# Output projection by seven block products, with the gate sums moved into an earlier stage

## The chip, the cores and the metric

One core of a Trainium2 chip runs the whole kernel. The metric is the device time of one execution in microseconds, as the median of several runs; the kernel before takes 1436.12 us (1434.32 to 1437.77 in three runs).

## The reference, cut to what matters

The program is one decoder layer over 512 tokens of width 2048 in float32. An input `x` is normalised, scaled and shifted, and multiplied by a large input matrix. Its columns feed two branches, a causal convolution and a differential attention; each is gated and projected back to 2048 columns. The branches are merged by sigmoid gates. What the change touches is the end:

```python
merged = sigmoid(m_conv) * y_conv + sigmoid(m_attn) * y_attn     # 512 x 2048
out = merged @ w_o                                               # 2048 x 2048
gate = (silu(c) @ w_ada + b_ada)[4096:]                          # 2048 values
x = x + gate * rms_norm(out, g_post)
```

`rms_norm` divides each token's row by the root of its mean square and multiplies it by `g_post`.

## The kernel before, in words

Every float32 operand of a matmul is split into a high and a low part (`split`, lines 143 to 151): ScalarE casts the high part, VectorE subtracts it from the operand. `mm3` (line 165) then issues three matmuls, high by high, high by low and low by high.

A scheduler turns the written program into a fixed order for each engine; an operation may move ahead of earlier written ones when its operands and its buffer are there. Only operations marked `ordered` keep their written order among each other on TensorE. Side work is written as generators in the list `work`; `pump` runs a number of their steps between the products of the main work, so that VectorE's side work is spread.

The stages that matter come in this order. In the cz, ma and mc stages (664 to 1072 us) `gemm_blocks` multiplies by columns of `w_in` with seven block products in place of eight (Strassen's method in Winograd's form): `s1`, `s2`, `s3`, `s4` are sums of weight blocks, `T1`, `T2`, `T3`, `T4` of token blocks. After each product it calls `pump` for one step. The ya and yc stages (1072 to 1247 us, `gemm_y`) project the attention and the convolution branch; yc merges and splits the result into `mgs`. The output stage (from line 926) multiplies `mgs` by `w_o`, 512 columns (`n`) at a time: four token tiles of 128 in four PSUM banks, sixteen steps of 128 in the inner dimension, three matmuls each. The last column block keeps half of its weights split in SBUF, so that the token tiles end one after the other; each is then squared and summed, multiplied by `gate * g_post`, scaled by its root mean square and added to `x`.

`gate(n)` (line 874) computes 512 gate columns: it loads 16 blocks of `w_ada`, two at a time, VectorE multiplies each by the column's `silu(c)` and adds it up, and a matmul with ones (`pgt`) sums over the partitions. Gate 0 is in the list during the yc stage, gates 1 to 3 during the output stage.

Buffers are pools with a fixed number of tiles: 27 pages of 512 columns (`page`), 12 tiles `temp`, 3 buffers each for 1 MB of raw weights (`wr`, also used for `x` at the end), high parts (`wh`) and low parts (`wl`), 2 `ws`. PSUM has eight banks: four `g`, two `s`, one `t`, one `o`. All loads and stores go through SP's queue, in its order.

Of the kernel before, what the change touches and what calls it, by code (L numbers as in the profile page):

```python
# [9 lines left out]
F32 = mybir.dt.float32  # L10
F32R = mybir.dt.float32r
# [5 lines left out]
P = 128  # L17
# [34 lines left out]
def hybrid_trunk(ctx: ExitStack, tc: tile.TileContext, x, c, w_ada, b_ada, g_pre, g_post, w_in,  # L52
# [17 lines left out]
    def page(name, dt=F32):  # L70
        return pp.tile([P, S], dt, tag="pg", name=name)
# [38 lines left out]
    def small(n, name):  # L110
        return sp.tile([P, n], F32, tag=f"sm{n}", bufs=1 if n > 16 else 8, name=name)
# [328 lines left out]
    def temp(name, dt=F32):  # L440
        return mp.tile([P, S], dt, tag="tmp", bufs=NTEMP, name=name)
# [305 lines left out]
    def conv_stats():  # L747
# [82 lines left out]
    def gemm_y(src, c0, rhs, name):  # L830
        ps = [gbank(f"py_{name}_{f}") for f in range(2)]
        raw = wraw(src, 0, 8, c0, 256, name)
        for q0 in (0, 4):
            whi, wlo = wsplit(raw[:, q0:q0 + 4, :], f"{name}_{q0}")
            for k in range(4):
                for f in range(2):
                    fs = slice(f * P, (f + 1) * P)
                    mm3(ps[f], (whi[:, k, fs], wlo[:, k, fs]), rhs[q0 + k], q0 + k == 0, q0 + k == 7)
        return ps
# [29 lines left out]
        fetch(f"yal{k}", lo.bitcast(F32))  # L869
        ya.append((hi, lo))  # L870
    work.append(conv_norm())
    gg = []

    def gate(n):

        bg = temp(f"bg_{n}")
        nc.sync.dma_start(out=bg, in_=b_ada2[2 * D + n * 512:2 * D + (n + 1) * 512].partition_broadcast(P))
        gp = page(f"gg_{n}")
        nc.sync.dma_start(out=gp, in_=g_post[0][n * 512:(n + 1) * 512].partition_broadcast(P))
        acc = page(f"accg_{n}")  # L880
        for k0 in range(0, KT, 2):
            raw = mp.tile([P, 2, S], F32, tag="ws", bufs=2, name=f"adag_{n}_{k0}")
            nc.sync.dma_start(out=raw, in_=ada_v[:, k0:k0 + 2, 2 * D + n * 512:2 * D + (n + 1) * 512])
            for k in range(2):
                s1 = cact[:, k0 + k:k0 + k + 1]
                if k0 + k == 0:
                    nc.vector.tensor_scalar_mul(acc, raw[:, k, :], s1)
                else:
                    nc.vector.scalar_tensor_tensor(acc, raw[:, k, :], s1, acc, op0=ALU.mult, op1=ALU.add)  # L889
            yield  # L890
        pgt = gbank(f"pgt_{n}", "gt"[n % 2])
        nc.tensor.matmul(pgt, ones, acc, start=True, stop=True)
        nc.vector.tensor_tensor(bg, pgt, bg, op=ALU.add)
        nc.vector.tensor_tensor(gp, gp, bg, op=ALU.mult)
        gg.append(gp)

    for j in range(8):
        py = gemm_y(w_attn_out[0], j * 256, ya, f"ya{j}")
        for f in range(2):
# [6 lines left out]
            mg.append(g)  # L906
        pump(YP)
    pump()
    mgs = []
    work.append(gate(0))  # L910
    for j in range(8):
        py = gemm_y(w_conv_out[0], j * 256, yc, f"yc{j}")
        for f in range(2):
            k = 2 * j + f
            g = temp(f"ga_{k}")
# [14 lines left out]
    def out_evac(n, t, ps):  # L930
        sq = temp(f"fsq_{n}_{t}")
        nc.scalar.activation(sq, ps, AF.Square, accum_out=fss[:, 4 * t + n:4 * t + n + 1])  # L932
        og[t][n] = page(f"og_{n}_{t}")
        nc.vector.tensor_tensor(og[t][n], ps, gg[n], op=ALU.mult)

    def out_mm(ps, t, k, w):
        mh, ml = mgs[k]
        ts = slice(t * P, (t + 1) * P)
        mm3(ps, (mh[:, ts], ml[:, ts]), w, k == 0, k == KT - 1)

    res = []
    zp = small(4, "fzp")
    for n in range(4):
        if n < 3:
            work.append(gate(n + 1))
        ps = [gbank(f"pw_{n}_{t}", ("gggg", "ssto")[n % 2][t]) for t in range(NT)]
        for q0 in range(0, KT, 4):
            raw = wraw(w_o[0], q0, 4, n * 512, 512, f"o_{n}_{q0}")
            for q1 in (0, 2):
                k0 = q0 + q1  # L950
                if n == 3 and k0 >= KT - RES:
                    for k in range(q1, q1 + 2):
                        hi, lo = page(f"woh_{q0 + k}", F32R), temp(f"wol_{q0 + k}", F32R)
                        split(raw[:, k, :], hi, lo)
                        res.append((q0 + k, (hi, lo)))
                    continue
                whi, wlo = wsplit(raw[:, q1:q1 + 2, :], f"o_{n}_{k0}")
                pump(1)
                for k in range(2):
                    for t in range(NT):  # L960
                        out_mm(ps[t], t, k0 + k, (whi[:, k, :], wlo[:, k, :]))
        pump()
        if n < 3:
            for t in range(NT):
                out_evac(n, t, ps[t])

    nc.vector.reduce_sum(zp, fss.rearrange("p (t n) -> p t n", n=4)[:, :, :3], axis=mybir.AxisListType.X)
    nc.vector.tensor_scalar(zp, zp, 1.0 / D, 4.0 * EPS, op0=ALU.mult, op1=ALU.add)
    for t in range(NT):
        for k, w in res:  # L970
            out_mm(ps[t], t, k, w)
        out_evac(3, t, ps[t])
# [3 lines left out]
        nc.vector.scalar_tensor_tensor(z, fss[:, 4 * t + 3:4 * t + 4], 1.0 / D, zp[:, t:t + 1],
                                       op0=ALU.mult, op1=ALU.add)
        r = rsqrt1(z, f"fr_{t}")
        for a, b in ((0, 2), (2, 3), (3, 4)) if t == NT - 1 else ((0, 4),):
# [34 lines left out]
```

## Time and profile before

| what | us |
|---|---|
| median of three runs | 1436.12 |
| profiled execution, its own time | 1436.9 |
| its span | 1435.1 |
| TensorE busy | 1397.3 |
| VectorE busy | 1080.9 |
| ScalarE busy | 522.1 |
| DMA read and written | 238.62 MB, 166 GB/s |

The span is the time from the first to the last recorded instruction. A share of busy time is an average over stages; what a change in a stage is worth is read from that stage. Matmuls overlap in the record, so the time of one in a row of them is taken from the length of the row.

### The profile page before, as it was taken

How to read it: one execution, taken by the hardware profiler on the slowest of the kernel's cores; microseconds unless marked ns; L12 is line 12 of the kernel's file. 1: busy time of each engine (PE TensorE's matmuls, PEld its weight loads, DVE VectorE, ACT ScalarE, POOL GpSimd, SP SyncE). 2: the span in 40 equal slices, each digit the busy share in tenths (PEclk: the TensorE clock that was granted, in tenths of full speed). 3: DMA queues.
4: the chain of work that ended last, by engine and by line, in shares of the span. 5: the costliest groups of instructions: out<-in, count | busy, mean ns of one | idle time of the engine just before them, and what ended most of it. 6: DMA issues, size and time to landing. Idle time of an engine off the chain costs nothing.

```text
span 1435.1 us, 20362 instructions
## 1 busy us (share of the span) xinstructions
PE 1397.3 (97%) x7999; PEld 1189.5 (83%) x7999; DVE 1080.9 (75%) x1750; ACT 522.1 (36%) x839; POOL 1.8 (0%) x8
## 2 busy tenths in 40 slices
PE   5899999999999999999999999999999999999997
PEld 4676787887777867788999999999998888888885
DVE  6997976988888887588988878777767676526645
ACT  3421333223433244444544444444445223222230
POOL 0000000000000000000000000000000000000000
PEclk9999999999999999999999999999999999999999
DMA  9888732331322322234635655543369875236544
GB/s 301 288 280 304 237 123 92 125 121 59 117 67 96 103 67 84 86 111 142 224 128 192 198 170 174 172 140 121 134 233 350 280 243 181 88 107 231 190 147 147
DMA packets 178338, 238.62 MB, mean 166 GB/s; under 512 B 8689, under 2 KB 119618, under 8 KB 177346
## 3 DMA queue, kind: packets, MB, share of 16 engines
q1 hardware_dynamic: 178242, 237.31, 49.9%
q8 instruction: 63, 1.03, 0.3%
q14 instruction: 33, 0.27, 0.1%
HBM read 210.02 MB, written 27.26 MB: 165 GB/s over the span
## 4 chain that ended last, share of the span: by engine, by line
PE 90%; DVE 5%; DMA 2%; ACT 1%; issue 1%; SPq 0%; DVEq 0%; ACTq 0%
PE pw L167 12%; PE pc L167 11%; PE py_ya L167 6%; PE py_yc L167 6%; PE pv L167 6%; PE pg_az L167 5%; PE pg_q L167 5%; PE pg_k L167 5%; PE x_ma L167 5%; PE x_mc L167 4%; PE z_ma L167 3%; PE y_ma L167 3%; PE y_mc L167 3%; PE z_mc L167 3%; PE x_cz L167 2%; PE y_cz L167 2%
## 5 line engine op out<-in xcount | busy, mean ns | idle before, releaser
L500 DVE SCALAR_TENSOR_TENSOR cacc<-u,cw,cacc 128x511 f32<-128x511 f32 (+14 forms) x240 | 164.4, 728 | 0.0
L167 PE MATMUL pc<-hp,wh_c 128*128 128x512 f32 x512 | 159.9, 397 | 3.0 <-DVE part L369 1.2
L167 PE MATMUL pw<-wh_o,mgs 128*128 128x512 f32 x448 | 140.6, 393 | 0.0
L167 PEld LDWEIGHTS pc<-hp,wh_c 128*128 128x128 f32 x512 | 95.6, 190 | 29.0 <-issue 2.7
L167 PE MATMUL pc<-hp,wl_c 128*128 128x512 f32 x256 | 99.0, 396 | 2.1 <-DVE wl_c L146 2.1
L167 PEld LDWEIGHTS pw<-wh_o,mgs 128*128 128x128 f32 x448 | 84.1, 188 | 18.9 <-ACT fsq L932 0.7
L167 PE MATMUL pw<-wl_o,mgs 128*128 128x512 f32 x224 | 87.2, 389 | 0.0
L369 DVE TENSOR_TENSOR part<-pc,part 128x512 f32<-128x512 f32 x96 | 64.7, 687 | 25.3 <-PE pc L167 25.0
L167 PE MATMUL pv<-wh_v,hp 128*128 128x512 f32 x256 | 82.8, 397 | 0.9 <-DVE part L369 0.9
L167 PE MATMUL pg_q<-hp,wh_q 128*128 128x512 f32 x256 | 82.7, 398 | 0.0
L167 PE MATMUL pg_az<-hp,wh_az 128*128 128x512 f32 x256 | 81.5, 395 | 0.0
L167 PE MATMUL pg_k<-hp,wh_k 128*128 128x512 f32 x256 | 80.1, 392 | 0.0
L167 PE MATMUL py_ya<-ya,wh_ya 128*128 128x512 f32 x256 | 78.7, 389 | 0.0
L146 DVE TENSOR_TENSOR wl_o<-wr_o,wh_o 128x1024 fp32r<-128x1024 f32 x28 | 34.2, 1222 | 52.7 <-ACT wh_o L145 52.7
L145 ACT CAST wh_c<-wr_c 128x1024 fp32r<-128x1024 f32 (+1 forms) x36 | 34.2, 955 | 104.0 <-DMA wr_c<-in_w_in_dram 54.9
L889 DVE SCALAR_TENSOR_TENSOR accg<-adag,cact,accg 128x512 f32<-128x512 f32 x60 | 45.1, 751 | 32.2 <-DMA adag<-in_w_ada_dram 31.1
L145 ACT CAST wh_o<-wr_o 128x1024 fp32r<-128x1024 f32 x28 | 29.5, 1052 | 104.5 <-PE pw L167 93.0
L167 PEld LDWEIGHTS pc<-hp,wl_c 128*128 128x128 f32 x256 | 48.5, 190 | 14.1 <-DVE wl_c L146 3.3
L167 PEld LDWEIGHTS pv<-wh_v,hp 128*128 128x128 f32 x256 | 47.8, 188 | 14.3 <-issue 4.5
L167 PEld LDWEIGHTS pg_az<-hp,wh_az 128*128 128x128 f32 x256 | 47.7, 188 | 12.0 <-issue 2.7
L167 PEld LDWEIGHTS pg_q<-hp,wh_q 128*128 128x128 f32 x256 | 47.2, 188 | 12.4 <-issue 2.8
L167 PEld LDWEIGHTS py_ya<-ya,wh_ya 128*128 128x128 f32 x256 | 48.0, 188 | 9.9
(333 smaller groups left out, 3695.0 us busy)
## 6 DMA issues: line engine op xcount, KB each, us to landing
ada<-in_w_ada_dram SPq DMA_DIRECT2D x128, 256.0 KB, 5.4
wr_ma<-in_w_in_dram SPq DMA_DIRECT2D x16, 1024.0 KB
wr_mc<-in_w_in_dram SPq DMA_DIRECT2D x16, 1024.0 KB, 5.2
adag<-in_w_ada_dram SPq DMA_DIRECT2D x32, 512.0 KB, 5.0
wr_o<-in_w_o_dram SPq DMA_DIRECT2D x16, 1024.0 KB, 5.1
wr_c<-in_w_in_dram SPq DMA_DIRECT2D x28, 512.0 KB, 6.1
wr_v<-in_w_in_dram SPq DMA_DIRECT2D x8, 1024.0 KB, 5.1
wr_q<-in_w_in_dram SPq DMA_DIRECT2D x8, 1024.0 KB, 5.0
```

Source lines behind the costliest of these rows:

```text
L145: nc.scalar.copy(hi, src)
L146: i = nc.vector.tensor_tensor(lo, src, hi.bitcast(F32), op=ALU.subtract)
L167: mm = nc.tensor.matmul(ps, a[p], b[q], start=start and i == 0, stop=stop and i == 2, skip_group_check=more)
L369: nc.vector.tensor_tensor(part[i], ps[f], part[i], op=ALU.add)
L500: paced(nc.vector.scalar_tensor_tensor(cvo[t][:, s:], u[t][:, :S - s], wj, cvo[t][:, s:], op0=ALU.mult, op1=ALU.add))
L889: nc.vector.scalar_tensor_tensor(acc, raw[:, k, :], s1, acc, op0=ALU.mult, op1=ALU.add)
```

## The change

The output projection is written as two groups of 1024 columns. In each, `w_o` and the merged activations are cut into 2 x 2 blocks (tokens in halves of 256, inner dimension in halves of 1024, columns in halves of 512), and seven block products give the four blocks of the result, in all eight banks. The token sums `T1` to `T4` are formed in the yc stage, whose column order becomes 0, 4, 1, 5, 2, 6, 3, 7; some of their splits are left for the start of the output stage (`late`). The weight sums are formed in the output stage. Results of columns 0 to 1023 are spilled to DRAM and fetched at the end. The gate sums load one 256 KB block at a time, one step ahead; gates 0 to 2 are in the list during the mc stage, gate 3 at the end of the ya stage, and their matmuls are `ordered`.

```diff
+    def gate(n):
+        raws = [None] * KT
+        def load(k):
+            if k < KT:
+                raws[k] = temp(f"adag_{n}_{k}")
+                nc.sync.dma_start(out=raws[k], in_=ada_v[:, k, 2 * D + n * 512:2 * D + (n + 1) * 512])
+        load(0)
+        yield
+        acc = temp(f"accg_{n}")
+        for k in range(KT):
+            load(k + 1)
+            s1 = cact[:, k:k + 1]
...
+                nc.vector.scalar_tensor_tensor(acc, raws[k], s1, acc, op0=ALU.mult, op1=ALU.add)
+            yield
...
+        pgt = gbank(f"pgt_{n}", "t")
+        ordered(nc.tensor.matmul(pgt, ones, acc, start=True, stop=True))
+        yield
+        nc.vector.tensor_tensor(bg, pgt, bg, op=ALU.add)
+        nc.vector.tensor_tensor(gp, gp, bg, op=ALU.mult)
...
+        if name == "mc":
+            work.extend(gate(n) for n in range(3))
...
+    work.append(gate(3))
...
-    for j in range(8):
+    for j in (0, 4, 1, 5, 2, 6, 3, 7):
         py = gemm_y(w_conv_out[0], j * 256, yc, f"yc{j}")
...
+            if k < KH:
+                b12[k] = g
+                u1 = t1[j][:, half]
+                nc.vector.tensor_tensor(u1, g[:, :H2], g[:, H2:], op=ALU.subtract)
+                split(g[:, :H2], hi[:, :H2], lo[:, :H2])
+                split(u1, hi[:, H2:], lo[:, H2:])
+                continue
             split(g, hi, lo)
+            t23 = temp(f"mt23_{kk}")
+            nc.vector.tensor_tensor(t23[:, :H2], g[:, H2:], t1[j - 4][:, half], op=ALU.add)
+            nc.vector.tensor_tensor(t23[:, H2:], b12[kk][:, H2:], g[:, H2:], op=ALU.subtract)
+            nc.vector.tensor_tensor(t4[:, half], g[:, :H2], t23[:, :H2], op=ALU.subtract)
...
-    for n in range(4):
-        if n < 3:
-            work.append(gate(n + 1))
-        ps = [gbank(f"pw_{n}_{t}", ("gggg", "ssto")[n % 2][t]) for t in range(NT)]
...
+    def oprod(ps, w, b, t, first, tiles=(0, 1)):
+        for k in range(2):
+            for i in tiles:
+                mm3(ps[i], b(2 * t + k, i), [v(k) for v in w], first and t + k == 0, t == 3 and k == 1,
+                    not first, ordered)
+        pump(1)
...
+    def x_again(t):
         xr = wp.tile([P, 4, 512], F32, tag="wr", name=f"xr_{t}")
         nc.sync.dma_start(out=xr.rearrange("p k n -> p (k n)"), in_=x2[t * P:(t + 1) * P, :])
+        return xr
...
+    work.append(late_splits())
+    for G in range(2):
+        c0 = G * 1024
...
+        for t in range(4):
+            ra = wraw(w_o[0], 2 * t, 2, c0, 1024, f"oa_{G}_{t}")
+            s1 = mp.tile([P, 2, S], F32, tag="ws", bufs=2, name=f"os1_{G}_{t}")
...
+            a11, a21 = ra[:, :, :S], ra[:, :, S:]
+            nc.vector.tensor_tensor(s1, a21, s1, op=ALU.add)
+            for k in range(2):
+                s2[2 * t + k] = temp(f"os2_{G}_{2 * t + k}")
+                nc.vector.tensor_tensor(s2[2 * t + k], s1[:, k, :], a11[:, k, :], op=ALU.add)
+            oprod(ox, wop_of(s2[2 * t:2 * t + 2], f"os2_{G}_{t}"), oT2, t, True)
+            oprod(oz, wop(a11, f"oa11_{G}_{t}"), oB11, t, True)
...
+            nc.vector.tensor_tensor(a21, a11, a21, op=ALU.add)
+            oprod(orr, wop(a21, f"os3_{G}_{t}"), oT3, t, True)
...
+            oprod(oy, wop(s1, f"os1_{G}_{t}"), oT1, t, True)
...
+        if G == 0:
+            for t in range(4):
+                rb = wraw(w_o[0], KH + 2 * t, 2, c0, 1024, f"ob_{G}_{t}")
+                a12, a22 = rb[:, :, :S], rb[:, :, S:]
+                oprod(oz, wop(a12, f"oa12_{G}_{t}"), oB21, t, False)
...
+                oprod(orr, wop(a22, f"oa22_{G}_{t}"), oT4, t, False)
...
+                oprod(oy, wop_of(s2[2 * t:2 * t + 2], f"os4_{G}_{t}"), oB22, t, False)
...
+            continue
+        for t in range(4):
+            a12 = mp.tile([P, 2, S], F32, tag="ws", bufs=2, name=f"oa12_{t}")
...
+            oprod(oy, wop_of(s2[2 * t:2 * t + 2], f"os4_{G}_{t}"), oB22, t, False)
...
+        for t in range(4):
+            rb = wraw(w_o[0], KH + 2 * t, 2, c0, 1024, f"ob_{G}_{t}")
+            a12, a22 = rb[:, :, :S], rb[:, :, S:]
+            if t < 2:
+                oprod(orr, wop(a22, f"oa22_{G}_{t}"), oT4, t, False)
+                oprod(oz, wop(a12, f"oa12_{G}_{t}"), oB21, t, False)
+            else:
+                held.append((t, [wop_of([a[:, k, :] for k in range(2)], f"{n}_{t}", t == 2)
+                                 for a, n in ((a22, "oa22"), (a12, "oa12"))]))
+            if t == 0:
+                for i in range(2):
+                    g = temp(f"oc12_{i}")
+                    nc.vector.tensor_tensor(g, oy[i], q[i], op=ALU.add)
+                    out_done(2, 2 + i, g, g, temp(f"osq12_{G}_{i}"))
+                    sums3(2 + i)
+                    finish(2 + i, x_again(2 + i))
+        for i in range(2):
+            xr = x_again(i)
+            for t, w in held:
+                oprod(orr, w[0], oT4, t, False, (i,))
...
+            for t, w in held:
+                oprod(oz, w[1], oB21, t, False, (i,))
+            out_done(2, i, oz[i], temp(f"oc11_{G}_{i}"), temp(f"osq11_{G}_{i}"))
+            finish(i, xr, ((0, 2), (2, 3), (3, 4)) if i else ((0, 4),))
```

`wop` and `wop_of` split a weight block into high and low parts in the `wh` and `wl` buffers (`wop_of` with its last argument set, into pages); `out_done` squares, sums and multiplies a finished block by the gate; `finish` scales a token tile, adds `x` and stores it.

## Rows read from the trace of the kernel before

**Rows 1.** the page, busy time of the engines; chain that ended last, by engine
```profile
PE 1397.3 (97%) x7999; PEld 1189.5 (83%) x7999; DVE 1080.9 (75%) x1750; ACT 522.1 (36%) x839; POOL 1.8 (0%) x8
...
PE 90%; DVE 5%; DMA 2%; ACT 1%; issue 1%; SPq 0%; DVEq 0%; ACTq 0%
```

**Rows 2.** chain that ended last, 1235 to 1436 us: start, us, what
```profile
1246.73 0.86 PE pgt L892 x2
1247.59 43.59 PE pw L167 x192
...
1381.04 43.72 PE pw L167 x192
1424.75 0.02 issue
```

**Rows 3.** busy time by stage: cz, mc, yc, output projection, tail
```profile
core 0: us, PE busy (x) PEld busy (x) DVE busy (x) ACT busy (x) POOL busy (x), PEclk, DMA share, GB/s
...
664.85:747.20 82.35, 82.35 (x685) 81.87 (x684) 73.97 (x106) 40.35 (x53) 0.00 (x0) 1.00 0.53 180
...
910.00:1072.60 162.60, 161.47 (x1345) 161.29 (x1345) 117.69 (x127) 71.27 (x90) 0.00 (x0) 1.00 0.46 154
...
1159.70:1246.70 87.00, 87.00 (x385) 72.03 (x385) 57.59 (x76) 25.01 (x31) 0.00 (x0) 1.00 0.53 176
1246.70:1424.80 178.10, 178.04 (x777) 145.19 (x775) 89.27 (x139) 42.62 (x67) 0.00 (x0) 1.00 0.45 151
1424.80:1435.10 10.30, 0.00 (x0) 0.00 (x0) 5.55 (x16) 0.66 (x2) 0.00 (x0) 0.69 0.72 290
```

**Rows 4.** what TensorE waited for, from 600 us: total, times, longest
```profile
PE x_mc L167 <- DVE tb_mc L718: 1.1, 1, 1.1
```

**Rows 5.** VectorE in order of time: start, duration, line, operation, shapes
```profile
983.82 0.42 DVE L718 TENSOR_TENSOR tb_mc<-x_mc,tb_mc 128x256 f32<-128x256 f32 x1
984.15 1.22 DVE L715 TENSOR_TENSOR wr_mc<-wr_mc 128x1024 f32<-128x1024 f32 x1
985.29 1.22 DVE L146 TENSOR_TENSOR wl_mc_s<-ws_mc,wh_mc_s 128x1024 fp32r<-128x1024 f32 x1
...
1249.78 0.68 DVE L146 TENSOR_TENSOR mgs<-ga,mgs 128x512 fp32r<-128x512 f32 x1
1250.38 0.68 DVE L894 TENSOR_TENSOR gg<-gg,bg 128x512 f32<-128x512 f32 x1
```

**Rows 6.** VectorE in order of time, finishing of token tile 0
```profile
1409.23 0.69 DVE L934 TENSOR_TENSOR og<-pw,gg 128x512 f32<-128x512 f32 x1 [19.05 <-ACT fsq L932]
1409.84 0.15 DVE L976 SCALAR_TENSOR_TENSOR fz<-fss,fzp 128x1 f32<-128x1 f32 x1
...
1411.75 2.74 DVE L982 SCALAR_TENSOR_TENSOR xr<-og,fr_y,xr 128x512 f32<-128x512 f32 x4
```

**Rows 7.** the page, groups by cost: count, busy, mean ns, idle before
```profile
L889 DVE SCALAR_TENSOR_TENSOR accg<-adag,cact,accg 128x512 f32<-128x512 f32 x60 | 45.1, 751 | 32.2 <-DMA adag<-in_w_ada_dram 31.1
```

**Rows 8.** SP's queue in order of time, from 1380 us
```profile
1386.39 3.87 SPq L974 DMA_DIRECT2D xr<-in_x_dram  x3
1414.52 0.34 SPq L983 DMA_DIRECT2D out_dram<-xr  x1
1419.10 0.33 SPq L974 DMA_DIRECT2D xr<-in_x_dram  x1
```

**Rows 9.** groups of ScalarE from 1247 us
```profile
L145 ACT CAST wh_o<-wr_o 128x1024 fp32r<-128x1024 f32 x26 | 27.4, 1052 | 97.4 <-PE pw L167 93.0 <-PE py_yc L167 4.4
```

**Rows 10.** the page, DMA issues: count, size, median us to landing
```profile
wr_o<-in_w_o_dram SPq DMA_DIRECT2D x16, 1024.0 KB, 5.1
```

**Rows 11.** busy time in stretches of 5 us, columns as in rows 3
```profile
125.00:130.00 5.00, 5.00 (x17) 2.57 (x16) 3.12 (x3) 0.00 (x0) 0.00 (x0) 1.00 1.06 396
...
135.00:140.00 5.00, 5.00 (x35) 4.76 (x33) 1.06 (x2) 0.00 (x0) 0.00 (x0) 0.84 1.07 372
140.00:145.00 5.00, 5.00 (x15) 4.14 (x16) 2.73 (x6) 2.37 (x4) 0.00 (x0) 0.50 0.50 175
```

More of the change, by code (lines that the diff above doesn't have):

```diff
@@ L798, in conv_stats @@
         crs.append(rs)
+    gg = [None] * 4
+    def gate(n):
[10 more added lines that the diff above has]
+            s1 = cact[:, k:k + 1]
+            if k == 0:
+                nc.vector.tensor_scalar_mul(acc, raws[k], s1)
+            else:
+                nc.vector.scalar_tensor_tensor(acc, raws[k], s1, acc, op0=ALU.mult, op1=ALU.add)
+            yield
+        bg = temp(f"bg_{n}")
+        nc.sync.dma_start(out=bg, in_=b_ada2[2 * D + n * 512:2 * D + (n + 1) * 512].partition_broadcast(P))
+        gp = page(f"gg_{n}") if n else dist
+        nc.sync.dma_start(out=gp, in_=g_post[0][n * 512:(n + 1) * 512].partition_broadcast(P))
+        yield
+        pgt = gbank(f"pgt_{n}", "t")
+        ordered(nc.tensor.matmul(pgt, ones, acc, start=True, stop=True))
+        yield
+        nc.vector.tensor_tensor(bg, pgt, bg, op=ALU.add)
+        nc.vector.tensor_tensor(gp, gp, bg, op=ALU.mult)
+        gg[n] = gp
+        yield
     crs = []
@@ L871, in hybrid_trunk @@
     work.append(conv_norm())
[L872 to L895, printed above, removed]
+    work.append(gate(3))
     for j in range(8):
@@ L908, in hybrid_trunk, with late_splits, late_page, get @@
     pump()
-    mgs = []
-    work.append(gate(0))
-    for j in range(8):
+    mB, mT1, mT23, mT4, late = [None] * KT, [None] * KH, [None] * KH, [None] * KH, []
+    b12, t1 = {}, {}
+    def late_splits():
+        for _, g, hi, lo in late:
+            split(g, hi(), lo())
+            yield
+    def late_page(box, i, name):
+        def get():
+            box[i] = page(name, F32R)
+            return box[i]
+        return get
+    for j in (0, 4, 1, 5, 2, 6, 3, 7):
         py = gemm_y(w_conv_out[0], j * 256, yc, f"yc{j}")
+        if j >= 4:
+            t4 = temp(f"mt4_{j}")
+        else:
+            t1[j] = temp(f"mt1_{j}")
         for f in range(2):
             k = 2 * j + f
+            kk, half = k % KH, slice(f * H2, (f + 1) * H2)
             g = temp(f"ga_{k}")
@@ new lines, in hybrid_trunk @@
+            split(g, hi, lo)
+            t23 = temp(f"mt23_{kk}")
+            nc.vector.tensor_tensor(t23[:, :H2], g[:, H2:], t1[j - 4][:, half], op=ALU.add)
+            nc.vector.tensor_tensor(t23[:, H2:], b12[kk][:, H2:], g[:, H2:], op=ALU.subtract)
+            nc.vector.tensor_tensor(t4[:, half], g[:, :H2], t23[:, :H2], op=ALU.subtract)
+            if kk < 4:
+                hi, lo = mT23[kk] = page(f"mt23h_{kk}", F32R), page(f"mt23l_{kk}", F32R)
+                split(t23, hi, lo)
+            else:
+                mT23[kk] = [None, None]
+                late.append((0, t23, late_page(mT23[kk], 0, f"mt23h_{kk}"), late_page(mT23[kk], 1, f"mt23l_{kk}")))
@@ L923, in hybrid_trunk @@
+        if j >= 4:
+            mT4[j - 4] = [None, None]
+            late.append((1, t4, late_page(mT4[j - 4], 0, f"mt4h_{j}"), late_page(mT4[j - 4], 1, f"mt4l_{j}")))
         pump(1)
     pump()
+    late.sort(key=lambda e: e[0])
     fss = small(16, "fss")
+    fz = small(4, "fzs")
     og = [[None] * 4 for _ in range(NT)]
[L930 to L942, printed above, removed]
-    for n in range(4):
-        if n < 3:
-            work.append(gate(n + 1))
-        ps = [gbank(f"pw_{n}_{t}", ("gggg", "ssto")[n % 2][t]) for t in range(NT)]
[L947 to L972, printed above, removed]
+    def part_of(pages, off):
+        def get(k, i):
+            return [p[:, off(k) + i * P:off(k) + (i + 1) * P] for p in pages(k)]
+        return get
+    oB11 = part_of(lambda k: mB[k], lambda k: 0)
@@ new lines, in hybrid_trunk @@
+    oT1 = part_of(lambda k: mB[k], lambda k: H2)
+    oT2 = part_of(lambda k: mT23[k], lambda k: 0)
+    oT3 = part_of(lambda k: mT23[k], lambda k: H2)
+    oT4 = part_of(lambda k: mT4[k // 2], lambda k: k % 2 * H2)
+    oB21 = part_of(lambda k: mB[k + KH], lambda k: 0)
+    oB22 = part_of(lambda k: mB[k + KH], lambda k: H2)
+    oz = [gbank(f"oz_{i}") for i in range(2)]
+    orr = [gbank(f"or_{i}") for i in range(2)]
+    ox = [gbank(f"ox_{i}", "s") for i in range(2)]
+    oy = [gbank(f"oy_{i}", "to"[i]) for i in range(2)]
@@ new lines, in oprod, with wop, wop_of @@
+    def oprod(ps, w, b, t, first, tiles=(0, 1)):
[4 more added lines that the diff above has]
+        pump(1)
+    def wop(raw, name):
+        whi, wlo = wsplit(raw, name)
+        return (lambda k: whi[:, k, :]), (lambda k: wlo[:, k, :])
+    def wop_of(parts, name, pages=False):
+        if pages:
+            his = [page(f"wph_{name}_{k}", F32R) for k in range(2)]
+            los = [page(f"wpl_{name}_{k}", F32R) for k in range(2)]
+        else:
+            hi = wp.tile([P, 2, S], F32R, tag="wh", name=f"wh_{name}")
+            lo = wp.tile([P, 2, S], F32R, tag="wl", name=f"wl_{name}")
+            his, los = [hi[:, k, :] for k in range(2)], [lo[:, k, :] for k in range(2)]
+        for k in range(2):
+            split(parts[k], his[k], los[k])
+        return (lambda k: his[k]), (lambda k: los[k])
@@ new lines, in out_done, with sums3 @@
+    def out_done(n, t, src, g, sq):
+        col = (0, 1, 3, 2)[n]
+        nc.scalar.activation(sq, src, AF.Square, accum_out=fss[:, 4 * t + col:4 * t + col + 1])
+        nc.vector.tensor_tensor(g, src, gg[n], op=ALU.mult)
+        if n < 2:
+            spill(f"og_{n}_{t}", g)
+        else:
+            og[t][n] = g
+    def sums3(t):
+        nc.vector.reduce_sum(fz[:, t:t + 1], fss[:, 4 * t:4 * t + 3], axis=mybir.AxisListType.X)
+        nc.vector.tensor_scalar(fz[:, t:t + 1], fz[:, t:t + 1], 1.0 / D, 4.0 * EPS, op0=ALU.mult, op1=ALU.add)
@@ L973, in hybrid_trunk, with finish @@
+    def x_again(t):
         xr = wp.tile([P, 4, 512], F32, tag="wr", name=f"xr_{t}")
         nc.sync.dma_start(out=xr.rearrange("p k n -> p (k n)"), in_=x2[t * P:(t + 1) * P, :])
+        return xr
+    def finish(t, xr, cuts=((0, 4),)):
         z = small(1, f"fz_{t}")
[L976 removed]
+        nc.vector.scalar_tensor_tensor(z, fss[:, 4 * t + 3:4 * t + 4], 1.0 / D, fz[:, t:t + 1],
                                        op0=ALU.mult, op1=ALU.add)
@@ L978, in hybrid_trunk @@
         r = rsqrt1(z, f"fr_{t}")
-        for a, b in ((0, 2), (2, 3), (3, 4)) if t == NT - 1 else ((0, 4),):
+        for a, b in cuts:
             for n in range(a, b):
```

48 lines of the change are left out of this document (46 added, 2 removed).

## The prediction

> **What bounds the kernel now.** I read the page's busy shares first: TensorE is busy 97% of the span, VectorE 75%, and the chain that ended last is 90% TensorE [rows 1]. A busy matmul engine could still be paced by others, so next the chain of waits over the last 200 us: the output projection is four stretches of 192 matmuls, each 43.6 to 43.7 us, with only the gate matmul pair (0.86 us) between them, and after the last matmul 10.3 us of chain to the end [rows 2]. So one 512-column matmul costs 43.59/192 = 0.227 us and nothing else sets the pace there. Then busy time by stage: in the mc stage TensorE works 161.5 of 162.6 us, in the output stage 178.0 of 178.1, VectorE 117.7 and 89.3 [rows 3]. The list of what TensorE waited for holds, from the mc stage on, one wait of 1.1 us [rows 4]. From there on this is a TensorE-bound kernel: a matmul taken out is time won, if VectorE, the buffers and the SP queue can feed the rest.
>
> **The change, part by part.**
>
> *Matmuls.* Before: 4 column blocks x 16 k x 4 token tiles x 3 passes = 768 matmuls. After: 2 groups x 7 products x 4 steps x (2 k x 2 tiles x 3 passes) = 672, of the same shape. 96 go: 96 x 0.227 = 21.8 us, all of it on the path. The four gate pairs remain (4 x 0.86), moved.
>
> The Trainium skill weighs on this term. The rows give 227 ns from matmul to matmul [rows 2]; "TensorE: Matmul & The Clock Gate", section "Back-to-back issue gap", gives about 131 ns for 512 columns in a sustained stream, which would make the 96 matmuls worth 12.6 us. The trace disagrees, and the measurement decides.
>
> *VectorE in the output stage.* Starts of back-to-back operations lie 1.14 us apart for 1024 columns, 0.60 for 512, 0.33 for 256 [rows 5]; I count by these, as durations overlap. First loops, 8 steps: five 1024-wide (two sums, three split subtractions) and four 512-wide: 40 x 1.14 + 32 x 0.60 = 64.8. S4 sums and splits: 32 x 0.60 = 19.2. The a12 and a22 splits: 14 x 1.14 + 4 x 0.60 = 18.4. Late splits 8 x 0.60 = 4.8. Evacuations, 18 per group: 36 x 0.60 = 21.6. Finishing a token tile takes 0.6 for the product, 1.9 for sum and root, 2.7 for four updates [rows 6]; its product is counted above, so 4 x 4.6, of which the last lies behind the matmuls: 13.8. Sum 143 us, beside 672 x 0.227 = 152.5 us of matmuls: VectorE goes from half loaded to 94%. It still fits, but waits can no longer hide everywhere.
>
> *Entry of the output stage.* The first product writes other banks than the last yc product and its operands fit the weight buffers (three) ahead of it: no gap. But the last yc column's evacuation (about 5.6 us: two times 4 x 0.60 and 3 x 0.33), the eight late splits and the first two steps meet here: 5.6 + 4.8 + about 14 us against 21.8 us of matmuls, part of it done earlier. Between 0 and 3 us; I take 1.
>
> *The yc stage.* VectorE is busy 57.6 of 87.0 us [rows 3]. Gate sums leave (up to 16 x 0.75 [rows 7]), block sums and splits come: 8 x 0.4 + 8 x 1.0 + 4 x 0.6 = 13.6. Hidden under py_yc matmuls; 0 us. Uncovered it would cost its 2 us of difference.
>
> *The gate in the mc stage.* Three gates put 48 accumulations (0.75 each [rows 7]; 0.67 to 0.75 when interleaved) and 6 x 0.60 there: 36 to 40 us on top of 117.7 of 162.6 [rows 3], so 153 to 157, 94 to 97%. All that SP issues more: 48 loads of 256 KB and 6 row loads, between two weight loads and two spills per 20 us, in order; a load behind a weight load that waits for its buffer waits too. Each gate's matmul pair has a fixed place between two products; if its sum is late, every later product queues behind it on TensorE, and nothing else is on that queue. Before, VectorE waited 31.1 us for gate data over 60 accumulations, 0.52 each, in a stage with room [rows 7]. Bounds: below nothing, no reason, since no matmul leaves this stage; 0 if the prefetch (now a step ahead, from a pool of twelve tiles) lands in time; above, 48 x 0.52 = 25 us more VectorE time, 178 to 182 against 162.6: 16 to 20 us lost. The nearest row is the cz stage: VectorE 74.0 of 82.4 us, 90%, also fed by loads one step ahead, and TensorE shows no idle time [rows 3]. I take 2.5. The fourth gate falls where the first fell before, at the end of the ya stage: 0.
>
> *The last section.* It starts with a step that I think is the costliest. The pool of 1 MB buffers has three. In the second group the order of requests is: first weight block of the last loop, then x for token tiles 2 and 3, then the other three weight blocks, then x for tiles 0 and 1. Before, x was asked for after all weights, and took all three buffers at once, 28 us ahead of the first output; the fourth x waited 4.6 us from the first output's issue for its buffer [rows 8]. So two of three buffers will hold x early, and weight block 1 must wait for block 0 to be split. Call T the end of the last S4 product. The three split buffers let block 0's second half be split only when the third S4 product ends, T - 2.7; cast 1.05 [rows 9] and subtraction 1.14 free the buffer at T - 0.5. Its successor's load lands 5.1 us later [rows 10], T + 4.6; cast and subtraction: T + 6.9. TensorE wants it at T + 5.4: 1.5 us late, and up to 3.5, since VectorE is then in the two finishes (2 x 5.2 us) that come first in program order. Block 2 gets a buffer when block 1 is split, about T + 8 to 10; landed and split T + 15 to 17, wanted after four products, T + 10.9 plus the delay so far: about 2.7 late. Block 3 follows an output transfer that frees a buffer (issued about T + 7 to 8, gone 4.6 to 8 later): split about T + 20, wanted one matmul group (1.4) after block 2: 2 late. Together 5 to 9; 0 if requests are served otherwise. I take 6.5.
>
> *Other traffic.* w_o is read 22 MB instead of 16 MB, og spilled and fetched (4 MB), while 12.6 MB of the gate's 16.8 MB leaves: the stage moved 151 GB/s at a DMA share of 0.45 [rows 3]; hidden, 0. The tail's form is unchanged: 10.3 us.
>
> **Sum.** The profiled execution took 1436.9 us (span 1435.1 and 1.8 around it): 1436.9 - 21.8 + 2.5 + 1.0 + 6.5 = 1425.1. It lies 0.8 above the median of the runs (1436.12), so 1424.
>
> **Rivals.**
>
> *Everything hides.* If buffers are granted otherwise than I think, or blocks land in time, and the mc stage behaves as cz did, at most 4 us are lost: 1436.1 - 21.8 + 2 = 1416 (1414 to 1418). For it: VectorE sums stay under TensorE's in every stage. Against: 94% twice, and a three-buffer pool with x in it.
>
> *VectorE becomes the bound in the mc stage (slower).* Gate data arrive late as they did before, VectorE stops 0.52 us at each of 48 accumulations, weight splits come late, products stall, at the upper bound by 20 us. With the last section's 6.5 and the entry's 1: 1436.1 - 21.8 + 20 + 7.5 = 1442. It decides as soon as all losses exceed 21.8, that is from 14 us here. For it: 97% nominal load and the recorded waits. Against: loads go out ahead, and the waits partly fall into idle stretches that exist anyway.
>
> *The clock falls in the last section.* Early in the kernel, some 10 us after a stretch with 17 matmuls in 5 us (22 of 0.227 us would fit), the granted clock went to 0.84 and then 0.50 (1.2 GHz), and 15 matmuls ran in 5 us [rows 11]. Stalls of 2 to 3 us in a row could bring that back; half of the last section's 21.8 us at half speed costs 11 us more: 1424 + 11 = 1435, no change. Against: the stalls are short, with dense matmuls between. The Trainium skill, "TensorE: Matmul & The Clock Gate", section "A second HAM failure mode: psum-queue depth-cycling", warns of a kernel that cycles through PSUM banks, as this one will at every twelve matmuls instead of every 192. By that rule the clock would swing throughout; in the mc stage, which changes banks every 24 shorter matmuls, it stood at 1.00 [rows 3], so the trace disagrees so far.
>
> *It does not do what it says*: 672 matmuls is counted from the loops, but if a block product starts late at each of the eight bank hand-overs by 2 to 3 us, the gain is spent: 1436. Nothing in the rows speaks for it.
>
> **How the numbers follow.** Forecast (1419 to 1431): 0.52. Everything hides: 0.25. VectorE bound in mc: 0.14. Clock: 0.05. Spent: 0.04. The likeliest case gives 1424. The low end 1414 is the saving alone (1436.1 - 21.8); the high end 1435 takes in the forecast with the mc step between its value and its bound and the others at their upper ends (1436.1 - 21.8 + 9 + 3 + 8 = 1434.3) and the clock case, and leaves out about 0.15 above and 0.03 below. A run of this kernel tells apart about 0.2%, 2.9 us. Faster by more than that, below 1433.2: 0.52 + 0.25 + 0.03 of the clock case = 0.80; within: 0.02 of it and the spent case = 0.06; slower: the mc case, 0.14.
>
> **What would show it.** Right: 672 matmuls in the output stage at 0.227 us, VectorE 90% or more busy there and in mc, three waits of 1 to 4 us on TensorE in the last 30 us for weight blocks 1 to 3, x loads issued ahead of these blocks. Wrong: TensorE waits of more than 8 us in the mc stage or ahead of a gate pair; no waits at all in the last section (then 1416); the granted clock under 1.00 after 1250 us.

## The result: 17 us slower, and the profile after

The changed kernel takes 1453.84 us (median of 4 runs, 1452.11 to 1457.88) against 1436.59 us for the kernel before in the same session (4 runs, 1434.32 to 1437.77): a ratio of 1.0126, 95% interval 1.0101 to 1.0151. The forecast of 1424 us and its range up to 1435 us are both missed, on the wrong side of the kernel before. The profiled execution has a span of 1451.6 us, 16.5 more than before.

The page first, busy time and the chain that ended last; these answer to [rows 1]:

```profile
PE 1387.0 (96%) x7903; PEld 1176.7 (81%) x7903; DVE 1175.2 (81%) x1916; ACT 558.8 (38%) x903; POOL 1.8 (0%) x8
...
PE 83%; DVE 9%; DMA 4%; ACT 1%; issue 1%; SPq 1%; DVEq 0%; ACTq 0%
```

96 matmuls are gone (x7999 to x7903), TensorE is busy 10.3 us less, and yet the span grew: TensorE now waits. Its share of the final chain fell from 90% to 83%, VectorE's rose from 5% to 9%. The busy time by stage says where; the columns are those of [rows 3], and the rows are mc, ya, yc, the hand-over from yc to the output stage, and its first and second group:

```profile
909.66:1074.17 164.51, 163.38 (x1350) 162.12 (x1349) 146.70 (x179) 71.21 (x89) 0.00 (x0) 1.00 0.66 221
1074.17:1172.64 98.47, 90.14 (x387) 73.34 (x387) 63.09 (x83) 34.01 (x42) 0.00 (x0) 0.97 0.80 274
1172.64:1260.00 87.36, 87.36 (x385) 71.97 (x385) 64.67 (x105) 27.46 (x42) 0.00 (x0) 1.00 0.39 135
1260.00:1269.20 9.20, 1.38 (x4) 0.45 (x2) 9.06 (x18) 4.24 (x7) 0.00 (x0) 0.78 0.00 0
1269.20:1343.40 74.20, 74.19 (x321) 61.35 (x322) 59.56 (x72) 34.01 (x48) 0.00 (x0) 0.98 0.45 152
1343.40:1434.90 91.50, 81.22 (x328) 64.37 (x327) 69.97 (x116) 37.27 (x60) 0.00 (x0) 0.94 0.56 199
```

Against [rows 3], and for ya (1072.6 to 1159.7 before, between the rows of mc and yc, 87.1 us):

| stage | before | after | difference | forecast |
|---|---|---|---|---|
| mc | 162.6 | 164.5 | +1.9 | +4.2 |
| ya | 87.1 | 98.5 | +11.4 | +0.9 |
| yc | 87.0 | 87.4 | +0.4 | +0.9 |
| output stage to its last matmul | 178.1 | 180.3 | +2.2 | -17.7 |
| tail | 10.3 | 11.3 | +1.0 | 0 |

The forecast is the prediction's terms with the four gate pairs of 0.86 us put where they moved: two into mc, one at the start of ya, one ahead of yc. The output stage has 672 matmuls x 0.2267 (twelve take 2.72 us) = 152.3 us of work, as counted, so it holds 28.0 us of idling and slow running. What TensorE waited for, from 600 us (total, times, longest; the groups under 1 us left out), against the one row of [rows 4]:

```profile
PE ox L167 <- ACT wh_os L145: 9.6, 2, 7.5
PE py_ya L167 <- ACT wh_ya L145: 8.3, 1, 8.3
PE or L167 <- ACT wh_oa L145: 3.3, 2, 3.0
PE or L167 <- DVE wl_oa L146: 2.0, 2, 1.8
PE ox L167 <- DVE wl_os L146: 1.5, 2, 1.2
PE x_mc L167 <- DVE wl_mc_s L146: 1.1, 1, 1.1
```

Four places hold nearly all of it. **The second weight block of ya** came late: 8.3 us. SP's queue in order of time (start, us, line, what) shows why:

```profile
1057.66 0.38 SPq L1064 DMA_DIRECT2D os<-in_w_o_dram  x1
...
1078.41 5.28 SPq L438 DMA_DIRECT2D cd<-scratch_cd  x8
...
1084.71 0.38 SPq L155 DMA_DIRECT2D wr_ya<-in_w_attn_out_dram  x1
```

Before, the second ya block was requested at 1057.64, right behind the gate loads. Now a 512 KB block of `w_o` for the output stage (`os`, line 1064) stands at that place, 174 us before its first use (a sum at 1231.49), because its `ws` buffer comes free at 1057.63, with a split of the mc stage that ends 16 us ahead of the stage itself; the ya block is requested only at 1084.71, behind eight `cd` fetches that take SP 5.28 us to issue.

**The entry of the output stage**: in the 9.20 us of the row of 1260.00 TensorE is busy 1.38. TensorE's two waits, in order of time (start, us, what, in brackets the idle time and what ended it):

```profile
1268.11 0.80 PE L167 MATMUL ox<-wh_os,mt23h 128*128 128x512 f32 x1 [7.52 <-ACT wh_os L145]
1269.21 0.80 PE L167 MATMUL ox<-wl_os,mt23h 128*128 128x512 f32 x1 [0.30 <-DVE wl_os L146]
```

VectorE around it, in order of time:

```profile
1231.49 1.23 DVE L1067 TENSOR_TENSOR os<-wr_oa,os 128x1024 f32<-128x1024 f32 x1 [0.51 <-DMA wr_oa<-in_w_o_dram]
...
1233.23 1.22 DVE L1079 TENSOR_TENSOR wr_oa<-wr_oa 128x1024 f32<-128x1024 f32 x1
...
1266.33 0.42 DVE L963 TENSOR_TENSOR mt<-ga,mt 128x256 f32<-128x256 f32 x1
1266.66 1.28 DVE L1070 TENSOR_TENSOR os<-os,wr_oa 128x512 f32<-128x512 f32 x2
```

The sums `s1` (line 1067) and `S3` (1079) of the first step are ready at 1232.7 and 1234.5. The sum `S2` (line 1070) of the same step, the operand of the first product `ox`, needs nothing later than `s1`, but is formed at 1266.66, behind the last yc evacuation (line 963 at 1266.33). It is the only one of the three that is written to a `temp` tile.

**The join of the two groups** repeats this at 1348.85 (waits of 2.10 and 1.18 us). **The last section**: `x` (`xr`) and weight blocks 1 to 3 (`wr_ob`) in SP's queue, in order of time:

```profile
1376.86 0.34 SPq L1041 DMA_DIRECT2D xr<-in_x_dram  x1
...
1387.20 0.34 SPq L1041 DMA_DIRECT2D xr<-in_x_dram  x1
...
1407.13 0.38 SPq L155 DMA_DIRECT2D wr_ob<-in_w_o_dram  x1
...
1416.80 0.38 SPq L155 DMA_DIRECT2D wr_ob<-in_w_o_dram  x1
...
1420.07 0.39 SPq L155 DMA_DIRECT2D wr_ob<-in_w_o_dram  x1
```

TensorE's longest waits there:

```profile
1415.56 0.79 PE L167 MATMUL or<-wl_oa,mt4h 128*128 128x512 f32 x1 [1.82 <-DVE wl_oa L146]
...
1428.51 0.50 PE L167 MATMUL or<-wh_oa,mt4h 128*128 128x512 f32 x1 [2.96 <-ACT wh_oa L145]
```

Two `x` tiles are requested 20 and 30 us ahead of weight block 1 and hold two of the three buffers, as the prediction said.

Around the ya wait the granted clock falls as well. Stretches of 5 us there:

```profile
1090.00:1095.00 5.00, 0.76 (x2) 0.50 (x2) 3.05 (x5) 3.19 (x4) 0.00 (x0) 0.61 1.08 364
1095.00:1100.00 5.00, 4.96 (x17) 3.64 (x16) 4.02 (x6) 2.91 (x5) 0.00 (x0) 0.71 1.08 364
```

In the stretch behind the wait TensorE is busy 4.96 of 5 us, but the row counts 17 matmuls, where a stretch at full pace counts 23 or 24 (clock 0.71, part of it at 1.2 GHz). The place costs 10.5 us in all, of which 8.3 are the wait.

### The profile page after: what moved, and what is told of

Its sections match the earlier page's. It is cut to its first block, busy times and chain, and to the rows that moved or that the text cites. A ratio compares the mean times of both kernels' runs of the same rounds, so it can differ in the third digit from the quotient of the medians.

```text
span 1451.6 us, 20533 instructions
## 1 busy us (share of the span) xinstructions
PE 1387.0 (96%) x7903; PEld 1176.7 (81%) x7903; DVE 1175.2 (81%) x1916; ACT 558.8 (38%) x903; POOL 1.8 (0%) x8
## 4 chain that ended last, share of the span: by engine, by line
PE 83%; DVE 9%; DMA 4%; ACT 1%; issue 1%; SPq 1%; DVEq 0%; ACTq 0%
PE pc L167 10%; PE pg_k L167 6%; PE py_yc L167 6%; PE pv L167 6%; PE py_ya L167 5%; PE pg_az L167 5%; PE pg_q L167 5%; PE x_ma L167 5%; PE x_mc L167 4%; PE z_ma L167 3%; PE y_ma L167 3%; PE y_mc L167 3%; PE z_mc L167 3%; PE x_cz L167 2%; PE oy L167 2%; PE oz L167 2%
## 5 line engine op out<-in xcount | busy, mean ns | idle before, releaser
L167 PEld LDWEIGHTS pg_k<-hp,wh_k 128*128 128x128 f32 x256 | 47.9, 188 | 9.4
L307 DVE SCALAR_TENSOR_TENSOR acc<-ada,cact,acc 128x512 f32<-128x512 f32 (+1 forms) x52 | 50.5, 970 | 1.6 <-DMA ada<-in_w_ada_dram 1.4
L167 PE MATMUL pg_k<-hp,wl_k 128*128 128x512 f32 x128 | 51.0, 399 | 0.0
L167 PE MATMUL pv<-wl_v,hp 128*128 128x512 f32 x128 | 50.6, 395 | 0.0
L167 PE MATMUL pg_az<-hp,wl_az 128*128 128x512 f32 x128 | 50.5, 396 | 0.0
L167 PE MATMUL py_ya<-ya,wl_ya 128*128 128x512 f32 x128 | 50.5, 394 | 0.0
```

The costliest lines, as they stand in the source:

```text
L307: nc.vector.scalar_tensor_tensor(acc, raw[:, kk - k0, :, :], cact[:, kk:kk + 1], acc, op0=ALU.mult, op1=ALU.add)
```

## Experiments

**Theory**: the 21.8 us are saved, and about 37 us are lost (10.5 in ya, 10 and 5.4 at entry and join, 11.2 in the last section) for three separate reasons: a request that moved in SP's order (ya), a sum that waits for a `temp` tile (entry and join), and `x` in the weight buffers (last section). Each loss is the delay of the next product against the pace of 0.2267 us: at the entry `oz` starts at 1273.14, while twelve matmuls of `ox` right behind the last yc product would have let it start at 1263.15. **Rivals**: the gate loads of the mc stage displace the ya block; VectorE, at 143 us in the output stage, is simply the bound, so that work put first makes other work late. Ratios are to the kernel before on the same chip; a difference of ratios times 1436 us gives microseconds.

### The small w_o blocks held back

```diff
+            with tc.issue_after(last_w[0].ins):      # the full weight block requested before
                 nc.sync.dma_start(out=s1, in_=w_o[0]...)
```

> Edit: the changed kernel, but the small w_o blocks of the first loop (os1) may be requested only behind the full weight block that precedes them. Theory (the early request of os1_0_0, whose buffer is free once the mc stage ends, took the place of the second ya weight block in SP's order, so that block was requested 27 us later): the wait of py_ya of 8.3 us goes, the ya stage falls from 98.5 to 88 to 90 us, the time from 1453.8 to about 1444 (1442 to 1447); entry of the output stage and last section unchanged. Rival (the gate loads of the mc stage fill the queue, and the second ya block is late because of them): wait of 6 to 9 us stays, time within 2 us of 1453.8.

1447.49 us, ratio 1.0082 (1.0067 to 1.0098): 6.3 us of the changed kernel's loss, against 10 expected. TensorE's wait for ya, of its list of waits:

```profile
PE py_ya L169 <- ACT wh_ya L145: 1.3, 1, 1.3
```

The stretches around it, columns as above:

```profile
1095.00:1100.00 5.00, 3.45 (x14) 2.15 (x13) 4.30 (x6) 3.94 (x5) 0.00 (x0) 0.94 1.08 365
1100.00:1105.00 5.00, 5.00 (x18) 4.01 (x17) 3.45 (x5) 2.29 (x3) 0.00 (x0) 0.72 1.08 366
```

The second block is in time. The wait of 1.3 us that is left is for the third one, requested at 1088.79 (before: 1081.94), also behind the `cd` fetches; and a wait of 1.3 us with the slow stretch behind it (18 matmuls in 5 us, clock 0.72) leaves the ya stage at 91.9 us, 4.8 above the 87.1 of before, 0.9 of it the gate pair. The rival about the gate loads fails for the long wait, and has part of the short one.

### The gate move alone

Edit: the kernel before with the new `gate`, three gates in the mc stage and the fourth in ya; the old output projection.

> Edit: the kernel before with the gate part of the change alone (three gates summed in the mc stage, the fourth in the ya stage, the old output projection without gate sums). Theory (the gate move costs about what the mc stage showed, 1 to 2 us, and does not delay the second ya weight block, since no w_o block is requested early here): 1436 to 1439, mc stage about 164.5 us, ya stage 87 to 89, no wait of py_ya above 2 us. Rival (the gate loads displace the second ya block): ya stage 96 to 99, time 1445 to 1448. Rival (the gates make VectorE the bound in mc): mc stage above 168.

1438.28 us, ratio 1.0011 (0.9997 to 1.0025): within what can be told from no change. A stretch of 164 us that takes in nearly all of the mc stage (it is 164.7 us long here), columns as above:

```profile
910.00:1074.00 164.00, 162.87 (x1344) 161.44 (x1344) 146.75 (x180) 70.60 (x88) 0.00 (x0) 1.00 0.65 219
```

VectorE is busy 146.75 of 164 us there (89%; the prediction had 94 to 97%) and TensorE has no wait above 1.1 us in mc. No `w_o` block is requested early here, and the second ya block is in time; the third is late by 1.4 us as in the run above, and the ya stage is 92.0 us (1075.51 to 1167.51), not 87 to 89: so the short wait belongs to the gate move, the long one doesn't. The output stage gives 4.0 us back (174.1 for its 768 matmuls, 178.1 with the gate pairs before). The profiled execution is one of the longest of the ten, so its stages add up to more than the median's 2.5 us.

### ya blocks first

```diff
+    first = [wraw(w_attn_out[0], 0, 8, j * 256, 256, f"ya{j}") for j in range(2)]
     mg, ya, yc = [], [], []
```

> Edit: the changed kernel, and only the first two weight blocks of the ya stage are requested before the ya pages; the early request of the small w_o block stays. Theory (what costs is that the second ya block stands late in SP's order, not the traffic of the small w_o block): as much gained as by holding the w_o block back, 5 to 8 us: 1446 to 1449. Rival (the small block's own 512 KB and the gate loads fill the DMA engines): less than 3 us gained.

1447.05 us, ratio 1.0086 (1.0065 to 1.0106): the same gain, with the early `w_o` block left where it was (requested at 1055.77, and the second ya block at 1058.04). It is the order in the queue that costs, not the 512 KB. Waits of 1.5 us for the third block and 0.7 us for a `ya` page are left in the stage.

### ox last in the first step

```diff
+            if t == 0:
+                oprod(oz, wop(a11, ...), oB11, t, True)
+                oprod(oy, wop(s1, ...), oT1, t, True)
+                nc.vector.tensor_tensor(a21, a11, a21, op=ALU.add)
+                oprod(orr, wop(a21, ...), oT3, t, True)
             for k in range(2):
                 s2[2 * t + k] = temp(f"os2_{G}_{2 * t + k}")
...
             oprod(ox, wop_of(s2[2 * t:2 * t + 2], ...), oT2, t, True)
+            if t == 0:
+                continue
```

> Edit: the changed kernel, with the order of the four products in the first step of each group turned round: oz, oy, or, and ox last, whose operand is the sum S2 held in a temp tile. Theory (ox came first and its sums waited for a temp tile that is freed only by the last evacuation before it; the other operands lie in the weight buffers): the excess at the entry of about 10 us falls to 1 to 3, that at the join of the groups from 5.4 to under 1, time 1453.8 to about 1440 (1438 to 1444). Rival (VectorE is simply bound there, whatever comes first): the wait moves to oz or oy at the same length, time within 3 us of 1453.8.

1440.58 us, ratio 1.0035 (1.0022 to 1.0047): 13 us come back from nothing but an order. All that TensorE still waits for at the entry, in order of time:

```profile
1267.52 0.50 PE L167 MATMUL ox<-wh_os,mt23h 128*128 128x512 f32 x1 [1.14 <-ACT wh_os L145]
1268.60 0.50 PE L167 MATMUL ox<-wl_os,mt23h 128*128 128x512 f32 x1 [0.58 <-DVE wl_os L146]
```

The stretch behind it:

```profile
1270.00:1275.00 5.00, 5.00 (x17) 3.95 (x17) 4.91 (x7) 4.12 (x6) 0.00 (x0) 0.70 0.69 252
```

Three products run at full pace before `ox`, the waits fall from 7.5 and 0.3 to 1.1 and 0.6 us, and those at the join are gone. VectorE has the same work as before, so the rival fails here.

### x behind the weight blocks

```diff
                     sums3(2 + i)
-                    finish(2 + i, x_again(2 + i))
+        for i in range(2):
+            finish(2 + i, x_again(2 + i))
```

> Edit: the changed kernel, with the two finishes of token tiles 2 and 3 and their loads of x placed behind the loop, so that all four weight blocks of the last section are requested before any x. Theory (two of the three 1 MB buffers were held by x, so weight blocks 1 to 3 came late): excess in the last section falls from 11.2 to 1 to 4 us, the tail after the last matmul may grow by up to 5 us since more finishing is left there; time 1453.8 to about 1446 (1443 to 1450). Rival (VectorE's finishing work delays the weight splits wherever x is): less than 3 us gained.

1445.12 us, ratio 1.0063 (1.0043 to 1.0083), 9 us gained. From its list of TensorE's waits every row of `or` has gone; SP's queue at the end, in order of time:

```profile
1414.12 5.42 SPq L1041 DMA_DIRECT2D xr<-in_x_dram  x3
1422.06 3.89 SPq L1053 DMA_DIRECT2D out_dram<-xr  x2
1429.73 0.34 SPq L1041 DMA_DIRECT2D xr<-in_x_dram  x1
```

All matmuls end at 1430.8, and 13.2 us follow (11.3 in the changed kernel): the fourth `x` is requested at 1429.73, when an output has freed its buffer, and VectorE's last updates wait 0.6 us for it.

### The three together, and two more

> Edit: the three edits together (small w_o blocks requested behind the full ones; ox last in the first step of each group; x of token tiles 2 and 3 after all weight blocks). Theory (three separate causes, each at its own place): the gains add up, 6.3 + 13.3 + 8.7 = 28.3 us: 1453.8 - 28.3 = 1425.5 (1422 to 1429), faster than the kernel before by about 10 us. Rival (one edit's gain is lost at the next place, since VectorE is the common bound): 1432 to 1440.

1423.59 us, ratio 0.9922 (0.9905 to 0.9938). The three gains alone are 6.3 + 13.1 + 9.0 = 28.4 us, together 0.0204 x 1436 = 29.3: they add up, so the three causes are separate, and the block products as such are worth having. Next the third ya block, requested with `for j in range(3)` behind the `ya` pages and ahead of `mg` and `cd`:

> Edit: the three edits together, and the first three weight blocks of the ya stage requested before the cd and mg loads (in SP's order the third one moves from behind cd_0 to cd_7 and tz_1 to ahead of them). Theory (the wait of 1.4 us for the third block that remains, and the stretch at a granted clock of 0.70 to 0.72 behind it, come from that block's place in SP's order): the ya stage falls from 91.8 to 87.5 to 89 us, 3 to 4 us less than the three edits alone. Rival (the DMA engines are full there, at shares of 1.06 to 1.08, and whatever is put first makes something else late): within 1 us of the three edits, with another wait of 1 to 3 us in the ya stage for ya, cd or mg.

1422.23 us, ratio 0.9913 (0.9893 to 0.9933). In the trace the ya stage is as forecast, with no wait and no slow stretch (the stage, then a stretch that was slow in the run above):

```profile
1073.50:1161.30 87.80, 87.80 (x386) 72.09 (x385) 61.43 (x82) 33.46 (x41) 0.00 (x0) 1.00 0.86 297
...
1100.00:1105.00 5.00, 5.00 (x24) 4.14 (x23) 3.94 (x7) 4.18 (x6) 0.00 (x0) 1.00 1.08 364
```

From its first product to the first one of yc the stage takes 88.3 us, against 91.9 in the run before it; the medians differ by 1.4 us only and their intervals overlap, so the gain is seen in the trace and not settled by the times. At the entry of the output stage this trace has the waits of the run before (1.1 and 0.6 us), but a granted clock of 0.66 from 1260 to 1265 us, where that run's stayed at 1.00. The DMA engines are as full as before (1.08), and nothing else became late. Then `x` of tile 2 in the two `ws` buffers:

> Edit: as the run before, and x of token tile 2 is loaded into the two 512 KB buffers that are free behind the last a12 block, so that three 1 MB buffers serve x of tiles 3, 0 and 1. Theory (with x last, the fourth x waited 3.7 us for an output transfer to free its buffer, was issued 0.7 us before the last matmul ended and landed 7.2 us later, so that the tail grew from 11.4 to 13.3 us): x of tile 1 is issued at least 5 us earlier, the tail falls to 10 to 11 us, 2 to 3 us less than the run before; about 1419 to 1421. Rival (the tail is VectorE's chain of the last two finishes): less than 1 us.

1422.33 us, ratio 0.9916 (0.9900 to 0.9933): nothing gained, a miss. The `x` loads are early (three requests from 1390.40), but VectorE's updates at the end stand as they did (in order of time):

```profile
1407.61 1.42 DVE L1064 SCALAR_TENSOR_TENSOR xr<-ogf,fr_y,xr 128x512 f32<-128x512 f32 x2
1408.94 1.41 DVE L1064 SCALAR_TENSOR_TENSOR xr<-oc,fr_y,xr 128x512 f32<-128x512 f32 x2
...
1412.78 1.42 DVE L1064 SCALAR_TENSOR_TENSOR xr<-ogf,fr_y,xr 128x512 f32<-128x512 f32 x2
```

Tile 0's four updates (1407.61 to 1410.3) and the root between stand ahead of tile 1's (1412.78): the tail of 12.7 us is VectorE's chain of two finishes, as the rival said.

### S2 in pages

```diff
-                s2[2 * t + k] = temp(f"os2_{G}_{2 * t + k}")
+                s2[2 * t + k] = (page if t == 0 and G == 0 else temp)(f"os2_{G}_{2 * t + k}")
```

> Edit: the changed kernel with its own order of products (ox first), but the two sums S2 of the very first step are written into pages of the large pool instead of temp tiles. Theory (at the entry these sums wait for a temp tile, not for VectorE or for w_o): they move ahead of the last yc columns' evacuations on VectorE, the wait of ox of 7.5 us goes, the entry's excess falls from 10 to 0 to 2 us, the join of the groups keeps its 5.4 us: 1453.8 - 9 = 1445 (1443 to 1448). Rival (VectorE has no room there: it is busy 9.06 of the 9.20 us of the gap, so whatever is done first, the same work must be done before TensorE can go on): less than 3 us gained, with the wait moved to the next products.

1450.64 us, ratio 1.0099 (1.0077 to 1.0121): 3.9 us gained, not 9. The theory's half came true: `S2` is formed at 1251.35, 15 us earlier, and `ox` starts on time at 1260.89. But then the third product waits, TensorE in order of time:

```profile
1269.99 0.79 PE L167 MATMUL or<-wh_os,mt23h 128*128 128x512 f32 x1 [2.82 <-DVE ga L948]
```

SP's queue, in order of time:

```profile
1247.99 1.64 SPq L438 DMA_DIRECT2D ga<-scratch_mc  x3
1263.54 0.38 SPq L155 DMA_DIRECT2D wr_oa<-in_w_o_dram  x1
1263.96 0.47 SPq L438 DMA_DIRECT2D ga<-scratch_mc  x1
```

The last fetch of the mc gates (`ga`), needed to finish the yc merge, is issued at 1263.96, behind a request for a weight block that waited 13.8 us for its buffer; in the changed kernel all four fetches went out at 1247.52. VectorE idles 2.4 us for it, so VectorE is not the bound here either: one full pool was exchanged for another place in SP's queue.

> Edit: the three edits and the early third ya block (as the fastest kernel so far, 1422.2), and the two sums S2 of the first step in pages. Theory (the 1.7 us wait of ox that remains at the entry, and the stretch at a granted clock of 0.70 behind it, are the rest of the same wait for temp tiles): 2 to 3 us less, 1419 to 1420.5. Rival (what is left there is VectorE's own backlog): within 1 us of 1422.2.

1420.46 us, ratio 0.9891 (0.9873 to 0.9909), the fastest of all: 33 us below the changed kernel and 14 to 16 below the kernel before. It lies 1.8 us below the 1422.23, with overlapping intervals, so neither the 2 to 3 us nor the rival's 1 us is settled by the times. What TensorE waited for from 900 us, without the 1.1 us of [rows 4]'s kind in mc:

```profile
PE ox L169 <- DVE wl_os L146: 1.2, 2, 0.7
...
PE oy L169 <- DVE oc L1098: 0.8, 1, 0.8
PE or L169 <- DVE ga L951: 0.6, 1, 0.6
```

A stretch at the entry:

```profile
1260.00:1265.00 5.00, 4.29 (x18) 2.89 (x16) 5.00 (x10) 4.61 (x8) 0.00 (x0) 1.00 0.56 213
```

At the entry VectorE is now busy 5.00 of 5.00 us: what is left there (0.6 + 0.5 + 0.7 us) is its backlog, as the rival said of the place. The granted clock stays at 1.00 through these shorter waits; but it did so too through the 1.2 and 0.6 us of the run with the three edits, so that their length is the reason is not shown.

## Why the prediction was wrong

**Right**: the rows that bound the kernel, 96 x 0.227 = 21.8 us, 672 matmuls at that pace, yc at nothing, and the mechanism of the last section with its three waits. The mc stage, priced at 2.5 us beside its two gate pairs, lost 0.2 (+1.9, of which the pairs are 1.7). VectorE's 143 us for the output stage meet the 142.98 measured between 1260.00 and 1440.30 closer than the count deserves: that stretch takes in 6.6 us of the last yc merge, and leaves out sums of `w_o` formed before it. It is luck too that the run with the three repairs ends at the forecast, at 1423.59: it has no waits in the last section, but 4.8 us more in ya, 4.5 us lost in the output stage and a tail 2.4 us longer. Of the signs named for being wrong, the granted clock under 1.00 after 1250 us came (0.78 in the row of 1260.00); of those for being right, VectorE's 90% didn't (89% in mc, 79% in the output stage).

**The step that failed most** is the entry, "The first product writes other banks than the last yc product and its operands fit the weight buffers (three) ahead of it: no gap." The operand of `ox` isn't a weight block but the sum `S2` in one of twelve `temp` tiles, which the late token sums and the last columns' merge still held. I priced the meeting of the two as VectorE time (0 to 3 us, 1 taken); it was 10 us of waiting and slow clock, as the run with `ox` last shows, and 5.4 more at the join of the groups, where the sum had no term at all.

**The second** is in the sentence on what SP issues more: I followed the new loads within the mc stage only, and put the fourth gate in ya at 0. The stage behind mc requests its own data through the same queue. Its second block lost its place to a `w_o` load into a `ws` buffer that comes free 16 us before mc ends, and its third to the gate loads: 10.5 us beside the gate pair. "w_o is read 22 MB instead of 16 MB ... hidden, 0" was right of the bytes and said nothing of the order.

**The third** is a size: the last section at 6.5, bounds 5 to 9. By the starts of TensorE's matmuls around these blocks it cost 11.2 us, and the run with `x` last gives 9.0 back while its tail grows by 1.9, which is 10.9. The first block was requested at T - 0.13 (forecast T - 0.5, with T = 1407.26), the next at T + 9.5 and T + 12.8, and the slow clock was not counted: the waits add up to 6.4 us (2.2, 1.0 and 3.2 for blocks 1 to 3, where 1.5, 2.7 and 2 were forecast, so their sum is luck in part), and the other 4.8 us are matmuls slower than 0.227 us behind them.

**The tail**, left at 10.3, became 11.3, and 12.7 to 13.2 once the stalls ahead of it were gone, since the finishes wait for VectorE.

The slower rival was put in the mc stage and priced at VectorE; the gate move alone shows that this price was near nothing. The rule about clock swings from changing banks ("TensorE: Matmul & The Clock Gate", section "A second HAM failure mode: psum-queue depth-cycling", in the Trainium skill), weighed with the clock rival, does not show here: with a bank change at every twelve matmuls the granted clock stood at 0.98 over the 74.2 us of the first group (0.80 in the 5 us behind the entry's wait, 1.00 from 1275 us on) and at 1.00 wherever nothing was late. The clock did fall, but only at waits. The clock rival's example [rows 11] was misread: from 136.29 to 141.02 us, around that fall, TensorE ran matmuls of one column, so it was no case of stalls among wide matmuls. The chance of slower, 0.14, was too low for a change that moves loads and sums between full pools and past other loads in one queue.

## What to carry to other kernels

When a change takes work off the bounding engine, list for every first product of a stage where its operand is stored and who holds that pool until then; VectorE's time was the smaller question here. A new load whose buffer is free early is issued early, and in a queue that works in order it takes the place of a load that is needed sooner: look at the request order of the stage in between as well as at bytes. Ask for the buffers that the next products need before those of the final step.

## What the runs showed of the hardware

A wait of TensorE can cost more than its length. In the changed kernel the waits of the four places add up to 25.8 of the 37.1 us lost; the other 11.3 us are matmuls that ran slower than 0.227 us behind them. For short waits the cost is uncertain, and their length doesn't settle it. Behind 1.3 us in ya, with the small `w_o` blocks held back, the granted clock was 0.72 for a stretch of 5 us (18 matmuls counted in place of 24). Waits of 1.1 and 0.6 us at the entry were followed by 0.70 with `ox` last, and by 1.00 in the run with the three edits (1.2 and 0.6 us). With the ya blocks first, a wait of 1.5 us, which ends at 1096.68, was followed by 1.00; the stretch that holds it and the one behind it:

```profile
1095.00:1100.00 5.00, 3.40 (x14) 2.40 (x14) 4.70 (x7) 2.71 (x3) 0.00 (x0) 1.00 1.08 364
1100.00:1105.00 5.00, 5.00 (x24) 4.14 (x23) 3.55 (x5) 4.62 (x6) 0.00 (x0) 1.00 1.08 366
```

What decides between the two is open. I had counted a wait at its length and the clock as a rival of its own, in the last section only.
